# Sliding windows copied by DMA alone: the 16 rows of a direct copy taken 7 windows apart

## The chip, the core and the metric

The kernel runs on one core of one Trainium2 chip. The metric is the device time of one execution in microseconds (us). Three timed runs of the kernel before gave 743.12, 743.45 and 745.0 us, median 743.45 us. One more execution was taken with the hardware profiler; its rows are what the prediction reads.

## The reference

The input has 32 batches of 4096 rows of 256 float32 numbers. Every batch is cut into windows of 64 rows, one window every 32 rows, so there are 127 windows, and neighbouring windows share half of their rows. Nothing is computed; everything is copied.

```
n_windows = (length - window_size) // stride + 1          # 127
for i in range(n_windows):
    start = i * stride
    result[:, i] = x[:, start:start + window_size].copy()
```

In units of the kernel, a block is 32 rows, 32 KB, and a batch of the input has 128 blocks (4 MB). Window w of a batch is the blocks w and w+1, 64 KB. A batch of the output has 127 windows, 254 blocks (8.3 MB). Neighbouring windows lie side by side in the output without a gap; in the input they overlap by one block.

## The kernel before

No compute engine works; all that the program does is to issue DMAs, from three engines, each with a queue of its own.

**Staged batches.** Every third batch (1, 4, ..., 31; 11 in all, line 143) is loaded whole into one of six SBUF tiles of 128 partitions by 32 KB and stored from there twice, once as the first half of each window and once as the second (`Staging`, lines 70 to 123). ScalarE issues these (`st.run(ring_s)`, line 173): six loads, then their twelve stores, then five loads, then their stores, the last batch's in smaller parts. A row of such a DMA is one block of 32 KB. The trace calls this queue q10.

**Direct batches.** The other 21 batches are copied from DRAM to DRAM without a stop in SBUF. SyncE issues these (queue q1). Lines 161 to 164 cut each direct batch into seven groups of 16 neighbouring windows: for a batch whose predecessor is staged they start at window 15, otherwise at window 0. That is 147 groups. Line 164 is the whole of it:

```
sixteens += [(b, w + 16 * j) for j in range((c.nw - w) // 16)]
```

The loop at line 175 issues them in this order, batch after batch. A group goes out as one DMA of 16 rows of 64 KB (line 187) or as two DMAs of 16 rows of 32 KB, the first halves of the windows and then the second halves (lines 183 and 184). Which it is, is set by a count kept in the loop (`share` and `turns`, lines 177 to 186): the halves come mostly while ScalarE loads, the whole rows mostly while it stores. There are 92 whole DMAs and 55 pairs of halves. SyncE issues them far ahead; nothing that it does in the loop waits for anything but room in the queue.

`windows` (line 29) writes both access patterns. The output's is `[[2 * blk, n], row]` and the input's `[[blk, n], row]`: n rows, one window apart on either side. Of the 16 rows of a group, the k-th starts k windows (64 KB) after the first one in the output, and k blocks (32 KB) after it in the input.

**What is left.** One single window (line 165) is issued in the middle of the loop. The 15 windows of each direct batch that no group takes (`edges`, line 166: windows 0 to 14 or 112 to 126) are issued by GpSimd on the software queue q0 (lines 192 to 200), after the last DMA but one of the main loop has landed (semaphore `near`, lines 176 and 192), each behind the last store of its neighbouring staged batches. Eleven windows of batch 30 are copied by `columns` in pieces of 4 KB (lines 200 and 203). Then SyncE waits for all semaphores (line 206).

Of the kernel before, what the change touches and what calls it, by code (L numbers as in the profile page):

```python
# [8 lines left out]
DIRECT, IN, OUT = 32768, 16384, 16384  # L9


class Copier:
# [13 lines left out]
    def oap(self, half_window, dims):  # L26
        return bass.AP(self.out.tensor, self.out.offset + half_window * self.blk, dims)

    def windows(self, q, b, w0, n, half=None, piece=DIRECT):

        blk = self.blk
        row = [1, 2 * blk if half is None else blk]
        h = half or 0
        return q.dma_start(  # L34
            out=self.oap((b * self.nw + w0) * 2 + h, [[2 * blk, n], row]),
            in_=self.xap(b * self.nb + w0 + h, [[blk, n], row]),
            max_dma_last_dim=piece,
        )

# [86 lines left out]
@with_exitstack  # L126
def kernel(
    ctx: ExitStack,
    tc: tile.TileContext,
    x: bass.AP,  # L130
    window_size: bass.AP,
    stride: bass.AP,
    out: bass.AP,
):
    nc = tc.nc
    W, S = int(window_size), int(stride)
    B, L, D = x.shape
    n_win = (L - W) // S + 1
    assert out.shape == (B, n_win, W, D)
    c = Copier(x, out, B, L, D, W, S, n_win)  # L140


    staged = [*range(1, B, 3)]
    items = [(b, -1 if b == B - 1 else 0, c.nb) for b in staged]
    place = {b: g for g, (b, _, n) in enumerate(items) if n == c.nb}
    direct = [b for b in range(B) if b not in staged]
    pool = ctx.enter_context(tc.tile_pool(name="xb", bufs=1))
    st = Staging(c, tc, pool, x.dtype, items, 6)
    ring_d, ring_s, ring_r = nc.sync, nc.scalar, nc.gpsimd
    done = tc.alloc_semaphore("done")  # L150
    near = tc.alloc_semaphore("near")
    rest = tc.alloc_semaphore("rest")
    total = {done: 0, near: 0, rest: 0}

    def count(dma, sem):
        dma.then_inc(sem, 16)
        total[sem] += 16

    sixteens = []
    for b in direct:
        w = 15 if b - 1 in staged else 0
        sixteens += [(b, w + 16 * j) for j in range((c.nw - w) // 16)]
    singles = [(B - 1, c.nw - 1, 1)]
    edges = [(b, 0 if b - 1 in staged else 112, 15) for b in direct[:-1]]
    last = B - 2
    edges.append((last, 112, 4))

    first_loads, loads, stores = 6 * 17, 5 * 17, 6 * 34  # L170
    turns = share = 0
    with tc.tile_critical():  # L172
        st.run(ring_s)

        for i, (b, w) in enumerate(sixteens):
            sem = near if i == len(sixteens) - 2 else done
            second = turns - first_loads - stores
            loading = turns < first_loads or 0 <= second < loads
            share += 120 if turns < 16 or -8 <= second < 16 else 90 if loading else 18
            if share >= 120:  # L180
                share -= 120
                turns += 4
                count(c.windows(ring_d, b, w, 16, 0), done)
                count(c.windows(ring_d, b, w, 16, 1), sem)
            else:
                turns += 3
                count(c.windows(ring_d, b, w, 16), sem)
            if i == len(sixteens) // 2:
                for b, w, half in singles:
                    count(c.windows(ring_d, b, w, 1, half, 2048), done)  # L190

        ring_r.wait_ge(near, 16)
        for b, w, n in edges:
            for k in (b - 1, b + 1):
                if k in place and b != last:
                    st.wait_stored(ring_r, place[k])
            count(c.windows(ring_r, b, w, n), rest)


        count(c.columns(ring_r, last, 116, 9), rest)  # L200
        ring_r.drain()  # L201
        st.wait_stored(ring_d, place[B - 1])
        count(c.columns(ring_d, last, 125, 2), done)
        total[st.ended] = st.count[st.ended]
        for sem, n in total.items():
            ring_d.wait_ge(sem, n)
# [35 lines left out]
```

## Time and profile before

| what | us |
|---|---|
| median of three timed runs | 743.45 |
| lowest and highest of them | 743.12, 745.0 |
| the profiled execution | 743.86 |
| its span, first to last recorded instruction | 742.1 |
| time around the span (743.86 - 742.1) | 1.76 |
| GpSimd's first edge DMA is issued at | 649.1 |

A DMA is carried out by 16 DMA engines, which serve all three queues. The trace records every packet that an engine moved: its queue, its start, its size and its duration. A block of 32 KB of a direct DMA is one packet, a block of a staged DMA is two packets of 16 KB, and the 4-byte packets are the increments of semaphores. Where the page gives the busy share of the DMA, 9 stands for 90% or more; where it gives the share of a queue, this is the time that its packets took, as a part of 16 engines times the span. The three shares need not stay under 100% together, as the records of two successive packets overlap a little.

### The profile page before, as it was taken

The page shows a single profiled execution, that of the slowest core. Times are in us where ns is not written, and L with a number is a line of the kernel's source. Part 1 is how long each engine was busy: PE and PEld are TensorE (multiplying, and loading weights), DVE is VectorE, ACT ScalarE, POOL GpSimd, SP SyncE. Part 2 cuts the span into 40 slices and gives each one's busy share as a digit, 9 for nine tenths or more (in the row PEclk, how much of TensorE's full clock was granted, in tenths as well). Part 3 has the DMA queues.
Part 4 walks back from the last instruction along what each step waited for, and adds up shares of the span by engine and source line. Part 5 has one row for each costly group of instructions (what it writes and reads, how often), then busy time and mean ns, then how long its engine had stood idle before and what let it go on. Part 6 is the DMA issues. An engine that isn't in the chain of part 4 may idle for free.

```text
span 742.1 us, 323 instructions
## 1 busy us (share of the span) xinstructions
POOL 12.7 (2%) x26
## 2 busy tenths in 40 slices
POOL 0000000000000000000000000000000000050100
DMA  8999999999999999999999999999999999999996
GB/s 361 424 430 427 435 431 428 423 435 425 428 427 426 428 428 420 429 435 427 427 427 412 433 435 431 427 436 432 434 424 429 430 424 426 428 435 432 421 420 253
DMA packets 18290, 313.26 MB, mean 422 GB/s; under 512 B 4336, under 2 KB 4336, under 8 KB 4528
## 3 DMA queue, kind: packets, MB, share of 16 engines
q1 hardware_dynamic: 8016, 154.32, 48.8%
q10 hardware_dynamic: 9104, 138.41, 44.0%
q0 software_dynamic: 1168, 20.51, 6.6%
q14 instruction: 2, 0.02, 0.0%
HBM read 220.95 MB, written 267.09 MB: 658 GB/s over the span
## 4 chain that ended last, share of the span: by engine, by line
another core or an unknown queue 92%; POOL 2%; issue 0%; POOLq 0%; SPq 0%
POOL out_dram L34 2%; POOLq L201 0%; POOLq L237 0%; SPq L172 0%; POOLq L114 0%
## 5 line engine op out<-in xcount | busy, mean ns | idle before, releaser
L34 POOL DMA_DIRECT2D out_dram<-in_x_dram x21 | 12.0, 575 | 685.4 <-DMA out_dram<-in_x_dram 648.7
L44 POOL DMA_DIRECT2D out_dram<-in_x_dram x1 | 0.6, 581 | 0.0
L223 POOL MEMSET const-float32-0.0<- 128x1 f32 x1 | 0.1, 98 | 0.2 <-issue 0.2
L223 POOL MEMSET const-bfloat16-1.0<- 128x1 bf16 x1 | 0.1, 101 | 0.0
L223 POOL MEMSET const-float32-1.0<- 128x1 f32 x1 | 0.1, 98 | 0.0
L223 POOL MEMSET const-uint8-127<- 128x1 uint8 x1 | 0.1, 98 | 0.0
## 6 DMA issues: line engine op xcount, KB each, us to landing
out_dram<-in_x_dram SPq DMA_DIRECT2D x92, 1024.0 KB, 99.8
out_dram<-xb ACTq DMA_DIRECT2D x21, 4096.0 KB, 138.5
out_dram<-in_x_dram SPq DMA_DIRECT2D x110, 512.0 KB, 90.2
xb<-in_x_dram ACTq DMA_DIRECT2D x10, 4096.0 KB, 130.5
out_dram<-in_x_dram POOLq DMA_DIRECT2D x20, 960.0 KB, 37.9
xb<-in_x_dram ACTq DMA_DIRECT2D x4, 1024.0 KB, 15.7
out_dram<-xb ACTq DMA_DIRECT2D x2, 1024.0 KB, 110.5
out_dram<-xb ACTq DMA_DIRECT2D x4, 512.0 KB, 94.4
```

The source lines that it names most:

```text
L34: return q.dma_start(out=self.oap((b * self.nw + w0) * 2 + h, [[2 * blk, n], row]), in_=self.xap(b * self.nb + w0 + h, [[blk, n], row]), m ...
L44: return q.dma_start(out=self.oap((b * self.nw + w0) * 2, [[part, 16], [2 * self.blk, n], row]), in_=self.xap(b * self.nb + w0, [[part, 16 ...
L223: nc = _bacc.Bacc("TRN2", target_bir_lowering=False, num_devices=1)
```

## The change

`windows` is given a factor `step` (1 if nothing is said) that widens the distance between rows on both sides. A direct batch still has seven groups of 16 windows. Group j now holds the windows w+j, w+j+7, w+j+14, ..., w+j+105 instead of w+16j to w+16j+15. Together the seven groups cover the same 112 windows. The k-th row of a DMA starts 7k windows (7k times 64 KB) after the first in the output and 7k blocks (7k times 32 KB) in the input. `apart` is 7 for every batch, both for w = 0 (127 // 16) and for w = 15 (112 // 16). The number of DMAs, their order, their shape, their choice of whole or halves, their semaphores and the queues are unchanged, as are the staged part, the single window, the edges and the columns.

```diff
-    def windows(self, q, b, w0, n, half=None, piece=DIRECT):
+    def windows(self, q, b, w0, n, half=None, piece=DIRECT, step=1):
...
-            out=self.oap((b * self.nw + w0) * 2 + h, [[2 * blk, n], row]),
-            in_=self.xap(b * self.nb + w0 + h, [[blk, n], row]),
+            out=self.oap((b * self.nw + w0) * 2 + h, [[2 * step * blk, n], row]),
+            in_=self.xap(b * self.nb + w0 + h, [[step * blk, n], row]),
...
-        sixteens += [(b, w + 16 * j) for j in range((c.nw - w) // 16)]
+        apart = (c.nw - w) // 16
+        sixteens += [(b, w + j, apart) for j in range(apart)]
...
-        for i, (b, w) in enumerate(sixteens):
+        for i, (b, w, apart) in enumerate(sixteens):
...
-                count(c.windows(ring_d, b, w, 16, 0), done)
-                count(c.windows(ring_d, b, w, 16, 1), sem)
+                count(c.windows(ring_d, b, w, 16, 0, step=apart), done)
+                count(c.windows(ring_d, b, w, 16, 1, step=apart), sem)
...
-                count(c.windows(ring_d, b, w, 16), sem)
+                count(c.windows(ring_d, b, w, 16, step=apart), sem)
```

## The prediction

> **What bounds the kernel now.** I read the page's queue table first, because no compute engine has work.
>
> ```profile
> span 742.1 us, 323 instructions
> DMA  8999999999999999999999999999999999999996
> GB/s 361 424 430 427 435 431 428 423 435 425 428 427 426 428 428 420 429 435 427 427 427 412 433 435 431 427 436 432 434 424 429 430 424 426 428 435 432 421 420 253
> q1 hardware_dynamic: 8016, 154.32, 48.8%
> q10 hardware_dynamic: 9104, 138.41, 44.0%
> q0 software_dynamic: 1168, 20.51, 6.6%
> HBM read 220.95 MB, written 267.09 MB: 658 GB/s over the span
> ```
>
> The three shares add to 99.4%: the 16 DMA engines are busy from the first slice to the last. Each queue moves its bytes at the same pace: 154.32 MB in 48.8% of 16 x 742.1 us is 26.6 GB/s for one engine, q10 gives 26.5 and q0 26.2. So the sum of all packets' durations, divided by 16, is the time. The chain of waits holds no engine that could be late; the chain is made of transfers:
>
> ```profile
> another core or an unknown queue 92%; POOL 2%; issue 0%; POOLq 0%; SPq 0%
> out_dram<-in_x_dram SPq DMA_DIRECT2D x92, 1024.0 KB, 99.8
> out_dram<-xb ACTq DMA_DIRECT2D x21, 4096.0 KB, 138.5
> out_dram<-in_x_dram SPq DMA_DIRECT2D x110, 512.0 KB, 90.2
> ```
>
> A direct DMA lands about 90 to 100 us after its issue, so SyncE is far ahead of the engines, and how long it takes to issue one is hidden behind these 90 us. The question is then only how long a packet takes. The packet records of the trace give it (ns; excess is the mean duration less the commonest one, summed over the packets and divided by 16 engines):
>
> ```
> queue  bytes  packets  commonest  mean    excess, us
> q1     32768  4704     1213       1223.3  3.0
> q10    16384  8448     611        617.8   3.6
> q0     32768  608      1213       1236.8  0.9
> ```
>
> With the start's and the small packets' the excess is 7.6 us, 1.0% of the span. The median of each row is its commonest value and nearly its minimum (1211 and 611): most packets run at a floor of 27.0 GB/s that is the same for direct packets and for 32-KB packets of the other queue. That floor is the engine's; I see nothing in the rows that an address could lower. What addresses can move is the excess.
>
> The view by stages (start, first stores, second loads, second stores, edges) shows how steady it is; the columns after the stretch are its length, GpSimd's busy time, the TensorE clock, the DMA share and GB/s:
>
> ```profile
> 0.00:27.00 27.00, 0.20 (x4) 1.00 0.92 379
> 27.00:290.00 263.00, 0.00 (x0) 1.00 1.01 428
> 290.00:428.00 138.00, 0.00 (x0) 1.00 1.01 427
> 428.00:649.00 221.00, 0.00 (x0) 1.00 1.00 429
> 649.00:742.00 93.00, 12.55 (x22) 1.00 0.93 393
> ```
>
> From the packet records the excess of these stages is 0.99, 2.30, 1.49, 1.10 and 1.67 us: 3.7%, 0.9%, 1.1%, 0.5% and 1.8% of each.
>
> **The change part by part.** Instructions: the changed program issues on SyncE the same 202 group DMAs in the same order with the same shapes (16 x 2 x 8192 and 16 x 8192), so 4704 packets of 32 KB and 16 increments for each DMA remain. Nothing is added or removed on ScalarE and GpSimd. Cost: 0, hidden by the 90 us lead. No wait is added. `near` still ends with the same DMA, and its time follows the engines' pace. If the lead were gone, SyncE's issue would still be 203 issues of a median 2.4 us (most of it waiting for room; the shortest took 0.56 us), 114 us at the shortest, beside 553 us of its loop.
>
> Placement: the rows of one DMA go to 16 engines. Do the engines really work on one DMA at the same time? At the end of the trace the last large packets of the engines end between 735.5 and 739.7 us, 4.2 us apart, which is less than two rows of a whole DMA (2 x 1.2 us of its own and about as much of q10 between). So yes, to within a DMA or two. Before, then, the 16 engines write one stretch of 1 MB and read one of 17 blocks, 0.5 MB; each block is read by two of them, half a row apart in time. After, they write rows spread over 106 windows, 6.9 MB, and read from 107 blocks, 3.5 MB. The second reading of a block now falls to the same engine, in the next DMA. Bytes read and written are unchanged.
>
> The trace of before has no DMA like this, so I bound it. **From below**: all direct excess gone is -3.0 us; if the staged and edge packets were slow only because of the direct ones, all of it goes, -7.6 us. There is nothing further, because of the floor. **From above**: the dearest full slice in the steady flow, the last but one, has 0.64 us of excess in 18.55 us, 3.5%; if the 622 us from 27 to 649 went from their 4.89 us (0.79%) to that, it would be +16.5 us. **Nearest rows**, two of them:
>
> - Staged rows. A DMA of q10 spans 4 MB of the input or 8 MB of the output, already as wide as the direct DMAs become. Its excess is 6.8 on 611, 1.11%; a direct packet's is 10.3 on 1213, 0.85%. The difference of 0.26% on q1's 362 us (48.8% of 742.1) is +0.95 us.
> - Edge rows. On q0 successive DMAs lie in different batches, so that engines which are out of step work megabytes apart. These are the same DRAM-to-DRAM packets of 32 KB, and they take 1236.8 instead of 1223.3 ns. It isn't a larger demand that makes them slow: from 649 to 723 us, 31.7 MB at 664 GB/s of HBM reading and writing (direct bytes counted twice) stand against 668 GB/s between 27 and 290 us. 13.5 ns x 4704 / 16 = +4.0 us. If the staged packets beside them also suffered as q10's do in that stage (0.74 us on 15.9 MB instead of 2.16 us on 118.0 MB), that is another 118.0 x (0.0465 - 0.0183) = +3.3 us.
>
> I take the edge rows: same kind of packet, both sides in DRAM, and spread. A staged packet has only one side there. So +4.0 us, with +0.95 and +7.3 as neighbours and -7.6 and +16.5 as ends.
>
> The sum: the profiled execution's 743.86 (742.1 of span and 1.76 around) + 4.0 = 747.9 us. Its time is 0.4 above the median of 743.45, so I predict 747.4 for a median.
>
> The Trainium skill has a rule that speaks against the change: "DMA: Bandwidth & Descriptors", section "Latency and other measured facts", row on the HBM row pitch, says that copies whose rows lie a large power of two apart slow down, 207 GB/s at 512 KiB, 164 at 2 MiB, 103 at 4 MiB against 214 for a padded pitch. The new pitch of 448 KB is close to its first figure in size, and by it direct packets would lose 214/207 - 1 = 3.4%, an estimate of +12 us, 756 us. But 448 KB is 7 x 64 KB and no power of two, and before had pitches of 64 and 32 KB, which are powers of two, with packets at the floor; by the rule as worded the sum gets nothing. No row here shows a pitch of 448 KB.
>
> **The rivals.**
>
> 1. *Nothing measurable.* Seven is odd, so the 16 rows have the same 16 different remainders by 1 MB as before, and address bits below that are spread exactly as they were. For it: the median packet is at the floor everywhere, and 88% of the direct packets are within 20 ns of it. Price by the staged rows, +0.95: 744.4 for a median; its own range is that of no change, 741.2 to 745.7.
> 2. *Faster: neighbours are what collides.* Two engines read each block 1.2 us apart, and 16 write into one MB; if these meet in the same part of the memory, the excess of q1 is theirs, and taking the rows apart removes it. Price: -3.0, 740.4; with all other excess -7.6, 735.9. It decides against my forecast as soon as the mean of q1's 32-KB packets falls under 1216 ns, or q10's falls with it, together over 2.2 us. Against it: between 427 and 538 us the same neighbours run with staged stores beside them with an excess of 0.01 us, so being neighbours isn't enough to be slow.
> 3. *Much slower: a collision of the 16 rows in step.* If the new pitch brings several rows to the same part of the memory, nothing dissolves it, as the engines stay in step. The price is that of the dearest slice, +16.5, 760. For it: HBM moves 658 GB/s, and no row shows how much is left. Against: the staged DMAs use wide spreads and are at the floor.
> 4. *The tail.* The engines share no barrier, so what one of them loses it keeps; the 4.2 us between the first and the last to end can shrink or double. It is part of all cases, at most 4 us either way.
>
> **How the numbers follow.** My forecast (a few us slower, own range 745.7 to 753): 0.39. Much slower: 0.06. Nothing measurable: 0.27. Faster: 0.28. About 0.3%, 2.2 us, is what a measurement of this kernel can tell from no change, so slower is 0.39 + 0.06 = 0.45, same 0.27, faster 0.28. The range runs from the end of the faster rival, 736, to that of the much slower one, 760, since both signs hold much of the chance and 0.2 may not be exceeded outside; I expect about 0.1 outside.
>
> **What would show it.** Right: the same 4704 packets with a commonest duration of 1213 ns and a mean near 1237; GB/s in the slices of the steady flow down by about 3 (0.6%); q1's share of the span equal or a little higher; `near`, which ends GpSimd's long wait at 648.7, 3 to 4 us later; the edge stage as long as before, 93 us. Wrong: q1's mean at 1223 or below with an earlier `near` (rival 2); a commonest duration above 1213, meaning the pace itself and not a few packets changed (rival 3); an unchanged `near` with a longer stage behind it (the tail). A count of packets other than 4704 would mean that I misread how the rows are cut.

## The result and the profile after

The changed kernel takes 750.13 us (median of 4 runs, 749.02 to 750.74), the kernel before, measured beside it, 743.64 us (4 runs). The ratio is 1.008, 95% interval 1.0067 to 1.0092. The profiled execution took 750.44 us, 6.6 us more than that of before, with a span of 748.7 us.

The page of the changed kernel, the same rows as were read of before:

```profile
span 748.7 us, 323 instructions
GB/s 364 420 443 425 425 427 425 433 418 418 412 430 418 421 425 414 421 430 416 416 427 409 430 435 427 427 433 431 426 413 421 423 421 420 414 431 429 429 422 267
q1 hardware_dynamic: 8016, 154.32, 49.2%
q10 hardware_dynamic: 9104, 138.41, 43.8%
HBM read 220.95 MB, written 267.09 MB: 652 GB/s over the span
out_dram<-in_x_dram SPq DMA_DIRECT2D x92, 1024.0 KB, 101.3
out_dram<-in_x_dram SPq DMA_DIRECT2D x110, 512.0 KB, 90.1
```

Packets and bytes are the same to the digit; only time is longer. The packet records (ns; excess in us, as in the prediction):

```
queue  bytes  packets  commonest  mean before, after   excess before, after
q1     32768  4704     1213       1223.3   1244.1      3.0    9.1
q10    16384  8448     611        617.8    620.0       3.6    4.7
q0     32768  608      1213       1236.8   1234        0.9    0.8
all                                                    7.6    14.7
```

The floor of 1213 ns stands; the share of direct packets more than 20 ns above it went from 12% to 26%. The excess grew by 7.1 us and the span by 6.6: the change is in these packets, 6.1 us of it in the direct ones.

Where in time? The landings of ScalarE's DMAs give the stages better than their issues do, since a DMA lands up to 169 us after its issue. Before, the first loads landed by 132 us, the first stores by 407, the second loads by 510, and the last DMA but one of the main loop at 649; after, by 131, 412, 515 and 656. First before, then after (the first two columns are the stretch and its length, the last two the DMA share and GB/s):

```profile
0.00:132.00 132.00, 0.20 (x4) 1.00 0.99 419
132.00:407.00 275.00, 0.00 (x0) 1.00 1.01 427
407.00:510.00 103.00, 0.00 (x0) 1.00 1.01 432
510.00:649.00 139.00, 0.00 (x0) 1.00 1.00 427
```

```profile
0.00:131.00 131.00, 0.20 (x4) 1.00 0.99 418
131.00:412.00 281.00, 0.00 (x0) 1.00 1.01 421
412.00:515.00 103.00, 0.00 (x0) 1.00 1.01 431
515.00:656.00 141.00, 0.15 (x1) 1.00 1.00 420
```

The stages of loads are as long as before, with the same GB/s. The two stages of stores lost 6 or 7 GB/s and are 5.5 and 2.0 us longer by the landings. The direct packets' mean went there from 1228 to 1255 and from 1223 to 1248 ns; in the second loads it is 1214 and 1215. (In the first loads it rose too, from 1220 to 1239, while the staged packets beside them went from 624 to 616, and the stage is as long as before.) GpSimd's wait for the main loop grew by the whole difference, and the edges behind it took 93.1 us instead of 93.3. Its wait, first before, then after:

```profile
POOL out_dram L34 <- DMA out_dram<-in_x_dram: 648.7, 1, 648.7
POOL out_dram L34 <- DMA out_dram<-in_x_dram: 655.4, 1, 655.4
```

### The profile page after: what moved, and what is told of

Read it like the earlier page. It is cut to its first block, busy times and chain, and to the rows that moved or that the text cites. A ratio compares the mean times of both kernels' runs of the same rounds, so it can differ in the third digit from the quotient of the medians.

```text
span 748.7 us, 323 instructions
## 1 busy us (share of the span) xinstructions
POOL 12.8 (2%) x26
## 4 chain that ended last, share of the span: by engine, by line
another core or an unknown queue 92%; POOL 2%; issue 0%; POOLq 0%; SPq 0%
POOL out_dram L34 2%; POOLq L202 0%; POOLq L238 0%; SPq L173 0%; POOLq L114 0%
```

## The experiments

Three theories stood at the start. W: the memory pays for write streams that lie far apart, since the cost stands where staged stores run. R: it is paid on the reading side. B: both sides count alike. All comparisons are with runs of the kernel before on the same chip (743.96, 743.71 and 743.47 us in the three sets).

**1 and 2. One side apart.** Each side is given a base and a distance of its own. For the writes apart:

```diff
-            in_=self.xap(b * self.nb + w0 + h, [[step * blk, n], row]),
+            in_=self.xap(b * self.nb + (w0 if side is None else side) + h, [[blk, n], row]),
...
-        sixteens += [(b, w + j, apart) for j in range(apart)]
+        sixteens += [(b, w + j, apart, w + 16 * j) for j in range(apart)]
```

and for the reads apart the same with the output's pattern.

> This kernel takes the 16 rows 7 windows apart in the output alone; the rows read stay neighbours, so the windows land in other places than the reference has them. Theory W (the memory pays for write streams that lie far from each other, which is why the cost stands only where staged stores run): the time of the changed kernel, 749 to 751 us, with a mean of q1's 32-KB packets near 1244 ns. Theory R (it is paid on the reading side, where neighbours shared blocks): the time of before, 743 to 744.5, mean near 1223. Theory B (both sides count alike): about 747, mean near 1233.

> This kernel takes the 16 rows 7 blocks apart in the input alone; the rows written stay neighbours, so the windows land in other places than the reference has them. W: 743 to 744.5 us and a mean of 1223 ns. R: 749 to 751 and 1244 ns. B: about 747 and 1233.

Writes apart: 743.7 us, ratio 0.9991 (0.9982 to 1.0). Reads apart: 749.94 us, ratio 1.0074 (1.006 to 1.0088). The mean of the direct packets was 1226 and 1242 ns. The pages, writes apart first:

```profile
span 741.9 us, 323 instructions
HBM read 220.95 MB, written 267.09 MB: 658 GB/s over the span
```

```profile
span 749.0 us, 323 instructions
HBM read 220.95 MB, written 267.09 MB: 652 GB/s over the span
```

The bytes are equal, and 652 is the changed kernel's own figure. W falls, and so does B: all of the cost that can be told from noise is on the reading side.

**3. Two apart.**

```diff
-        apart = (c.nw - w) // 16
-        sixteens += [(b, w + j, apart) for j in range(apart)]
+        for step in (2, 2, 2):
+            sixteens += [(b, w + j, step) for j in range(step)]
+            w += 16 * step
+        sixteens += [(b, w, 1)]
```

> 96 of the 112 windows of a batch go 2 apart, the other 16 are neighbours. If the cost grows with the distance of the rows (16 rows over 1.9 MB instead of 6.9 MB), about a sixth of the 6.5 us: 744 to 745.5 us. If only the loss of direct neighbours counts, 6/7 of it: 748.5 to 750. If it is the distance of 7 in itself (a meeting of certain address bits), nothing: 743 to 744.5, which this run alone would not tell from the first.

744.9 us, ratio 1.001 (1.0 to 1.0021). In 96 of the 112 windows the rows of a DMA no longer share blocks, and almost nothing is lost, so it isn't that neighbours had the second reading of a block for less.

**4. Another order of the groups.**

```diff
-        sixteens += [(b, w + j, apart) for j in range(apart)]
+        sixteens += [(b, w + j, apart) for j in (0, 2, 4, 6, 1, 3, 5)]
```

> Still 7 apart, but the seven groups of a batch go out in the order 0, 2, 4, 6, 1, 3, 5, so an engine no longer reads a block at the end of one row and again at the start of the next. If this re-reading by one engine costs (or saves) something, the time moves from 750.1 towards 743.6 (or above 752). W and B: no change, 749 to 751 us, mean near 1244 ns.

750.19 us, ratio 1.0076 (1.0061 to 1.0091), mean 1241 ns: no change from the changed kernel. How soon a block is read again doesn't matter here.

**5, 6, 11, 12. Other distances.** What was left is the distance of the rows read: does the cost grow with it?

```diff
-        apart = (c.nw - w) // 16
-        sixteens += [(b, w + j, apart) for j in range(apart)]
+        sixteens += [(b, w + j, 4) for j in range(4)]
+        sixteens += [(b, w + 64 + j, 3) for j in range(3)]
```

> 64 of the 112 windows go 4 apart, 48 go 3 apart. So far only the distance of the rows that are read counts: 2 apart cost 0.94 us for 96 windows, 7 apart 6.2 to 6.5 us. Theory D (the cost grows evenly with the distance of the rows read): 1.1 us for each window of distance beyond the first, mean distance beyond the first 2.57, so +2.8 us, 746 to 747.5, mean of q1 near 1233 ns. Theory P (7 is bad in itself): 744 to 745.2, as with 2. Theory S (a step: free up to some width, then the full price): either 744 to 745.2 or 749 to 751.

The others are the kernel with the reads apart with another distance (8, 4, 6) in the input's pattern; the seven bases stay w+j.

```diff
-            in_=self.xap(b * self.nb + w0 + h, [[step * blk, n], row]),
+            in_=self.xap(b * self.nb + w0 + h, [[(1 if step == 1 else 8) * blk, n], row]),
```

> The rows read are 8 blocks apart (256 KB), the rows written neighbours, so the windows hold other blocks than the reference's. D: about as with 7 on the reading side and a little more, 750 to 752 us. P, if it is the address bits: a power of two brings rows together that 7 keeps apart, so far slower (over 755), or it is 7 that is bad and 8 is back at 743 to 745. S: as with 7, 749 to 751.

> As the run with the rows read 8 apart, with 4: the whole kernel, neighbours written, windows hold other blocks than the reference's. X and E: little, 743.5 to 745.5 us, as with 8 (745.3) and with 2. D2: between 2 and 7, about 747.

> The same with 6. X: as with 7, 748 to 750.5 us. E: as with 8, 744 to 745.8. D2: about 749.

```
rows read apart            us      ratio    95% interval       excess of q1, of q10, us
1 (before, in its profile) -       -        -                  3.0   3.6
2 (96 of 112), both sides  744.90  1.0010   1.0000 to 1.0021   4.9   3.1
8, reads alone             745.26  1.0017   1.0008 to 1.0026   5.1   2.8
4, reads alone             747.10  1.0044   1.0031 to 1.0056   5.5   3.9
4 and 3, both sides        747.27  1.0042   1.0029 to 1.0056   6.8   3.1
7, reads alone             749.94  1.0074   1.0060 to 1.0088   8.5   5.7
6, reads alone             755.75  1.0153   1.0139 to 1.0168   12.2  8.3
```

D2, E and X in the expectations are the theories that were left after the run with 8: D2, that the distance counts after all; E, that odd distances above 1 are bad; X, that 1, 2, 4 and 8 are cheap and the others dear.

With 4 and 3 the even growth (D) seemed right: 747.27 against 746 to 747.5 expected. With 8 it fell: 745.26 where it wanted 750 to 752. The profiles of 8 and then of 6, the mildest and the worst of the distances tried on the reading side alone:

```profile
span 742.8 us, 323 instructions
HBM read 220.95 MB, written 267.09 MB: 657 GB/s over the span
```

```profile
span 755.8 us, 323 instructions
q1 hardware_dynamic: 8016, 154.32, 49.1%
HBM read 220.95 MB, written 267.09 MB: 646 GB/s over the span
```

Two blocks less between the rows make 13.0 us of span, with the same program otherwise. E falls with 6. D2 has 4 right (747.10 against about 747), but 6 costs far more than the 749 it allowed, and more than 7. X has the order right, 2, 4 and 8 each costing less than 6 and 7, but not the sizes: 4 cost more than the 745.5 it allowed, and 6 far more than its 750.5. The kernels with 4, 6 and 8 also read other blocks than the one with 7, some more often and some less often or not at all; the bytes are the same, but that part isn't separated. So the address pattern of the reads sets the cost, and its width alone doesn't; the rule behind the numbers is open.

**7 and 8. Whole rows or staged stores?** The cost stood in the stages of stores, where the direct groups mostly go out whole. The condition `share >= 120` was replaced by `True` (all halves) and by `False` (all whole), still 7 apart.

> 7 apart as in the changed kernel, but every direct group goes out as two DMAs of half windows, in the stages of staged stores too. The cost stood in the stages of stores, where the groups go out whole; this separates the two. If staged stores beside them make the direct reads dear: q1's mean in the stages of stores stays at 1240 to 1260 ns. If it is the whole rows of 64 KB: it falls to about 1215 to 1225. The time is not compared, since the queues' shares shift: between 745 and 765 us.

> 7 apart, every direct group whole, in the stages of loads too. If staged stores matter: q1's mean in the second stage of loads stays near 1215 ns. If the whole rows matter: it rises there to 1245 to 1255. The time is not compared, since the queues' shares shift: between 745 and 765 us.

With halves the staged stores cost nothing: q1's mean is 1216 ns from 127 to 368 us and 1213.6 from 470 to 650, both beside stores. With whole rows it is 1261 in both stages of loads, more than the 1245 to 1255 expected, where the changed kernel's second has 1215. First halves (first stores, and second stores up to 650 us), then whole (the two stages of loads):

```profile
127.00:368.00 241.00, 0.00 (x0) 1.00 1.01 431
470.00:650.00 180.00, 0.00 (x0) 1.00 1.01 431
```

```profile
0.00:152.00 152.00, 0.20 (x4) 1.00 0.99 406
442.00:564.00 122.00, 0.00 (x0) 1.00 1.00 413
```

So staged stores are not what makes it dear. (The times of 758.79 and 764.68 us say nothing on this: with halves the staged stores run dry at 677 us and the edges are left alone; with whole rows the main loop ends at 635 and ScalarE's stores are left over.) But the form also sets how the two queues share the engines, and with it how much the memory is asked for. A direct byte is read and written in HBM, a staged one only read or written. By the packet records, in GB/s, where "asked" is 16 engines at the floor (32768 bytes in 1213 ns each, 432 GB/s) times one plus the direct share, and "moved" what HBM did in the stage:

```
stage                          direct share  asked  moved  mean of q1, ns
7 apart, halves, first stores  51.5%         655    653    1216
after, second loads            52.9%         661    659    1215
before, first stores           57.0%         679    670    1228
after, first stores            57.2%         679    661    1255
7 apart, whole, second loads   58.5%         685    654    1261
```

Where no more than about 660 is asked, it is delivered within 2 GB/s; where more is asked, less comes, and in the two stages at 57% the rows' distance decides how much. Form and share move together in these five rows, but the ends of the same two runs part them:

```
stage                                            direct share  asked  moved  mean, ns
all halves, last stores, 660 to 675 us           73%           748    678    1401 (q1)
all whole, edges beside stores, 646 to 694 us    57%           680    680    1221 (q0)
```

Halves are dear too once the staged stores run dry and the direct share rises. And the edges, which are whole rows of neighbouring windows on q0, get all that they ask for at a share at which the whole rows 7 apart did not. So the form doesn't make the packets dear by itself. As I read it, it acts through the share, and the distance decides what the share costs. These are short stretches (131 and 363 direct packets), the edges run on another queue, and no run held the share and changed the form alone; the step from share to memory stays argued.

**9 and 10. The direct groups alone**, all whole, with a distance for each batch: ScalarE's and GpSimd's parts are taken out, and

```diff
-        apart = (c.nw - w) // 16
-        sixteens += [(b, w + j, apart) for j in range(apart)]
+        r, o = kinds[direct.index(b)]
+        at = lambda j, s: w + (j if s > 1 else 16 * j)
+        sixteens += [(b, at(j, o), o, at(j, r), r) for j in range(7)]
```

> This kernel leaves out the staged batches, the edges and the columns: only the 147 direct groups run, all as whole DMAs, alone. The distance of the rows changes from batch to batch: read 1, 7, 8, 2, 3, 6, 4, 5 apart with neighbours written, the same eight again, then 7 apart on both sides, written alone 7 apart, the same two again, and 1. So windows hold other blocks than the reference's. DRAM to DRAM alone counts every byte twice in HBM, so if the memory is the limit the packets are far over their floor of 1213 ns: in the end of the run with all halves one queue alone got 261 to 341 GB/s, which for 154 MB would be 450 to 590 us. Theory X (with 1, 2, 4, 8 the 16 rows fall evenly on the memory's parts, other distances let some meet): batches at 3, 5, 6, 7 read slower than those at 1, 2, 4, 8. Theory E (odd distances over 1 are bad): 3, 5, 7 slower, 6 as 2, 4, 8. Theory D2 (distance after all, and the run with 8 is odd for some other reason): slower from 1 to 8 in order. If the engine's own pace is the limit, all batches equal at 27 ns a KB less overhead.

> The same batches alone, the distances in reverse order over the batches, so that a distance and a place in the memory are told apart: what belongs to the distance follows it. Theories as for the run before: X 3, 5, 6, 7 slow; E 3, 5, 7 slow; D2 in order of the distance.

472.92 and 474.2 us, within the 450 to 590 expected of a memory limit. (The engine's own pace would be 1213 ns for 32 KB, 38 ns a KB; the expectation's 27 is a slip, it is the floor of 27 GB/s.) The page of the first:

```profile
span 471.1 us, 196 instructions
q1 hardware_dynamic: 7088, 154.18, 99.1%
HBM read 154.17 MB, written 154.17 MB: 654 GB/s over the span
```

The engines are as busy as ever, 99.1%, but they move 327 GB/s instead of 422: the packets took 1583 ns on average, and HBM moved 654 GB/s, 653 in the second run. I read this as waiting for the memory. A queue that has the engines to itself isn't slow for that reason: in the run with all whole rows only staged stores run from 718 to 726 us, and their packets take 611 ns, the floor. It isn't excluded that an engine copies from DRAM to DRAM at a slower pace when no staged packets come between. Nor is 654 a ceiling: the first stores of before moved 670, and the edges in the table above 680. The kernel before moves about as much all the time (658 over its span). As to the distances, the two runs settle little: the mean packets over all batches of a kind are 1549 ns for 1, 1568 written 7 apart, 1570 for 8, 1573 for 4, 1581 for 3, 1585 for 7 on both sides, 1592 for 7, 1597 for 6, 1618 for 2, 1626 for 5, and single batches of one kind differ by up to 79 ns. Neighbours are the fastest in both runs, writes apart cost little; but 2, cheap in the whole kernel, is dear here, so none of X, E and D2 gives this order.

## Why the prediction was right, and where not

**The bound and the floor: right.** 4704 packets and a commonest duration of 1213 ns stayed, and the time came in the excess. Issue cost nothing.

**The placement term: right in sign, small by a third.** The step "the mean of q1's packets goes from 1223 to 1237" gave +4.0 us. It went to 1244, +6.1 us. The staged packets beside them, priced at nothing in the forecast and at +3.3 as the outer value, lost 1.1. The excess grew by 7.1 and the time of the profiled execution by 6.6; the median of 750.13 us is 2.7 us above the 747.4 forecast, within its own range of 745.7 to 753.

**The reason for the term: wrong.** I took the edge rows because they lie megabytes apart, and let the width of the whole DMA, 6.9 MB written and 3.5 MB read, carry the price. The runs show that width isn't it. The 6.9 MB on the writing side cost nothing (0.9991), and a wider reading with 8 costs a quarter of what 7 does (1.5 us of 6.0). The edge rows were hardly slow for their width either. I compared the demand from 649 to 723 us, but took the packets' mean over the whole stage. In those 74 us q0's packets took 1228 ns, which would have priced the term at about +1.5 us; the 75 of 608 packets after 723 us lifted the mean to 1236.8, as they took 1298 while direct packets had 65% of the bytes. So the number was near by luck: the price came from packets slowed, as I read it, by a larger direct share, not from rows that lie apart. What does slow the reads at 7 apart, and not at 8, stays open.

**Rival 1** argued that odd distances keep the address bits below 1 MB spread as before, so that nothing could change. Half of it, the writes, came true. On the reading side it failed with 7.

**Rival 2** fell: neighbours were the best of all reading distances tried, 2 apart hardly worse (1.0010, 1.0000 to 1.0021). My argument against it was a misreading, though. I dated the stages by ScalarE's issues and took 427 to 538 us for staged stores; by the landings, the second loads last until 510. From 510 to 538 us staged stores do run beside the neighbours, at a direct share of 57%, and the packets take 1213 ns there too. So 28 us are left of the argument, and over the whole second stores the mean of before is 1223.

**Rival 3** asked whether the memory has something left, and said that no row showed it. Experiments 9 and 10 show 654 GB/s for direct copies alone, and no stretch of the table above moved more than 680, so, as far as these runs show, little was left above the 658 of before. Three quarters of its price of +16.5 us was reached by a distance of 6 (+12.3), not by 7.

**The tail** was right at nothing: the edges took 93.1 us, and `near` moved by 6.7 us where I expected 3 to 4, the same shortfall as in the term.

The pitch rule of the Trainium skill ("DMA: Bandwidth & Descriptors", section "Latency and other measured facts") names large powers of two as the slow pitches. Here, on the reading side, the powers of two were the milder ones: 256 KB (8 blocks) 1.0017, against 1.0074 at 224 KB and 1.0153 at 192 KB. The pitches are smaller and the rows fewer than in its measurement, so it isn't refuted, but a distance is not safe because it is no power of two.

## What to carry to other kernels

When all DMA engines are busy all the time, look at the packets' durations beside their commonest value: here the floor of 1213 ns stood in every run, and only the excess moved when addresses moved. Count a DRAM-to-DRAM byte twice and compare each stage with what the memory was seen to give; where that was reached here, the distance of the rows read decided up to 1.5%, and which distance is bad had to be measured, for reads and writes apart. When a row is taken as a price, take its mean from the same stretch as the conditions that it is compared by. Date the stages by landings, not by issues, when a queue runs 100 us ahead.

## What the runs showed of the hardware

- Direct copies alone moved 326 to 327 GB/s, 653 to 654 GB/s of HBM reads and writes together, at packets of 1583 to 1585 ns on average, while the same packets beside staged transfers mostly run at 1213.
- Rows written 7 windows apart (448 KB) cost nothing (0.9991, 0.9982 to 1.0); rows read 7 blocks apart (224 KB) cost 0.74%, 6 apart (192 KB) 1.5%, 8 apart (256 KB) 0.17%. Why these differ stays open.
- The staged packets can suffer with the direct ones, though nothing of theirs was changed: with 6 apart their excess rose from 3.6 to 8.3 us.
- Beside staged stores, direct DMAs of half rows took 51.5% of the bytes (all halves, 127 to 368 us), of whole rows 58.4% (all whole, 152 to 442 us): the size of a row changes how the queues share the engines.
